# Layer 3's ConvFFN: fourteen of its twenty-two ktiles of up-projection as 2x2 blocks in seven products

## The chip, the core and the metric

The kernel runs on one core of a Trainium2 chip, in one launch. The metric is the device time of one execution in microseconds (us), lower is better. An execution's time is compared as a median over runs; the profile shows one further execution, instruction by instruction.

## The reference

Four layers work on 640 tokens (512 sample, 128 prompt) of 1024 features, each a token mixer and a gated ConvFFN, each of these followed by a LayerNorm. The change lies in the ConvFFN of layer 3, the last sub-layer of the program:

```python
def _conv_ffn(h, w_up, conv_w, conv_b, w_down):
    a, b = jnp.split(h @ w_up, 2, axis=-1)
    ap = jnp.pad(a, ((0, 0), (1, 1), (0, 0)))
    a = ap[:, :-2] * conv_w[0] + ap[:, 1:-1] * conv_w[1] + ap[:, 2:] * conv_w[2] + conv_b
    return (jax.nn.gelu(a) * b) @ w_down
```

`h` is 640 x 1024, `w_up` 1024 x 5632 (2816 for `a` and 2816 for `b`), `w_down` 2816 x 1024. The convolution runs over the tokens of each group for itself. All is float32.

## The kernel before

**Layout.** Features lie on the 128 partitions, tokens along the free dimension. A ktile is 128 features: 1024 features are 8 ktiles, the 2816 of the FFN are 22. Tokens are worked in halves, half 0 = tokens 0 to 256 and half 1 = 256 to 640 (in the very last projection 0 to 384 and 384 to 640).

**Split operands.** A float32 product is made of float32r parts: each operand is held as (hi, lo), and `mm3` (L175 to L177) issues three matmuls per ktile of the contraction, hi·hi (L175), hi·lo (L176) and lo·hi (L177), adding up in PSUM. Weights come by `unit`: SyncE's queue (SP) loads 512 KB into one of four buffers `raw`, ScalarE (ACT) casts it to the hi part (L163), VectorE (DVE) subtracts for the lo part (L164), both into one of six buffers `hl`:

```python
nc.scalar.copy(hl[:, 0], r)                                  # L163
(e or nc.vector).tensor_sub(hl[:, 1], r, hl[:, 0])           # L164
```

Activations are split in the same way by `split` (L169, L170).

**The FFN.** Ktile j of the up-projection needs two pieces of weights (2j for `a`, 2j+1 for `b`), each a contraction over 8 ktiles of h. `up(j)` makes four products: `a` of half 0 and 1, copied by ACT into a padded buffer `ap` (`ffn_a`, L500 to L503), and `b` of half 0 and 1. `ffn_g` then does the convolution (one ACT pass, L512, and two DVE passes, L514, for the sample and for the prompt each), gelu on ACT (L516), the product with `b` read from PSUM (DVE, L518 and L519) and the split of the result g. Of the first six ktiles half 0 is made earlier, in `ffn_pre`, while the LayerNorm of half 1 is still at work; `skew` makes their half 1, from ktile 5 down to ktile 0. Then `up(6)` and on. The down-projection runs in three chunks of ktiles, 0 to 7, 7 to 14 and 14 to 22: a chunk's `down` comes behind the first ktile of the next chunk, and the last chunk's `project` ends the program with the LayerNorm and the stores.

**What sets the order.** A scheduler places the instructions of this code when the program is built, by priority and by a model of durations; what comes out is one fixed list for each engine, which the engine works off in order, each instruction waiting on semaphores for what it reads and for the buffer that it writes. Buffers are handed on in pools: a new tile of `hl` takes the buffer of the oldest one, once all who read that are done. No DMA of the kernel before is issued from GpSimd's queue (POOL); every load goes through SP.

Of the kernel before, what the change touches and what calls it, by code (L numbers as in the profile page):

```python
# [1399 lines left out]
```

## Time and profile before

| | us |
|---|---|
| median of 3 runs (2803.19 to 2812.57) | 2807.13 |
| span of the profiled execution | 2805.7 |
| layer 3's ConvFFN: `skew`, from about | 2363 |
| its `up` and `down` in between | 2412 to 2738 |
| last chunk, LayerNorm and stores to | 2806 |

The profiled execution's own span is 1.4 us under the median. The page gives the busy time of each engine over the span; PE is TensorE's matmuls, PEld its weight loads, DVE VectorE, ACT ScalarE, POOL GpSimd. In a timeline an instruction stands with its start, its duration, the shapes, and in brackets how long the engine had been idle before it and what it waited for. Matmuls are pipelined: the distance between two starts is what one costs, the duration shown is from issue to the modelled end. "PEclk" in a table by windows is TensorE's granted clock as a share of full speed (1.00 is 2.4 GHz, 0.50 is 1.2 GHz).

### The profile page before, as it was taken

The page shows a single profiled execution, that of the slowest core. Times are in us where ns is not written, and L with a number is a line of the kernel's source. Part 1 is how long each engine was busy: PE and PEld are TensorE (multiplying, and loading weights), DVE is VectorE, ACT ScalarE, POOL GpSimd, SP SyncE. Part 2 cuts the span into 40 slices and gives each one's busy share as a digit, 9 for nine tenths or more (in the row PEclk, how much of TensorE's full clock was granted, in tenths as well). Part 3 has the DMA queues.
Part 4 walks back from the last instruction along what each step waited for, and adds up shares of the span by engine and source line. Part 5 has one row for each costly group of instructions (what it writes and reads, how often), then busy time and mean ns, then how long its engine had stood idle before and what let it go on. Part 6 is the DMA issues. An engine that isn't in the chain of part 4 may idle for free.

```text
span 2805.7 us, 46039 instructions
## 1 busy us (share of the span) xinstructions
PE 2749.6 (98%) x17826; PEld 2636.0 (94%) x17826; DVE 1973.0 (70%) x4263; ACT 1240.0 (44%) x2286; POOL 407.5 (15%) x417
## 2 busy tenths in 40 slices
PE   7999999999999999999999999999999999999998
PEld 4799999999989999999978999999799999999998
DVE  6879977857697887777587878775756558534344
ACT  5656232336496752323367423234532248423233
POOL 1250000024303300000442000005100042000003
PEclk9999999999999999999989999999999999999999
DMA  7735644432402445455104554542422224322221
GB/s 241 259 109 163 198 154 149 156 121 80 134 22 83 136 153 158 149 157 153 56 35 150 151 165 151 158 136 80 161 65 91 68 62 152 97 82 68 83 75 54
DMA packets 99932, 344.70 MB, mean 123 GB/s; under 512 B 11392, under 2 KB 14080, under 8 KB 99584
## 3 DMA queue, kind: packets, MB, share of 16 engines
q1 hardware_dynamic: 99712, 341.74, 38.7%
q8 instruction: 141, 2.31, 0.3%
q14 instruction: 79, 0.65, 0.1%
HBM read 336.19 MB, written 2.88 MB: 121 GB/s over the span
## 4 chain that ended last, share of the span: by engine, by line
PE 88%; DVE 5%; issue 2%; ACT 2%; DMA 2%; POOL 1%; POOLq 0%; ACTq 0%; SPq 0%; DVEq 0%
PE mm L175 26%; PE mm L176 26%; PE mm L177 26%; PE mm L487 2%; PE st L352 1%; PE mm L1157 1%; DVE hl L164 1%; DVE tmp L339 1%; DMA raw<-in_wmod 1%; PE mm L1247 1%; PE bc L372 1%; DVE lnt L383 1%; DVE act L170 0%; PE mm L1072 0%; DMA raw<-in_wup 0%
## 5 line engine op out<-in xcount | busy, mean ns | idle before, releaser
L177 PE MATMUL mm<-act,hl 128*128 128x384 f32 (+2 forms) x4928 | 1528.5, 310 | 3.2 <-DVE hl L164 3.2
L175 PE MATMUL mm<-act,hl 128*128 128x384 f32 (+2 forms) x4928 | 1531.5, 311 | 0.0
L176 PE MATMUL mm<-act,hl 128*128 128x384 f32 (+2 forms) x4928 | 1528.6, 310 | 1.2 <-POOL act L418 1.2
L177 PEld LDWEIGHTS mm<-act,hl 128*128 128x128 f32 x4928 | 935.1, 190 | 5.0 <-DVE hl L164 4.4
L176 PEld LDWEIGHTS mm<-act,hl 128*128 128x128 f32 x4928 | 935.9, 190 | 3.7 <-POOL act L418 1.8
L175 PEld LDWEIGHTS mm<-act,hl 128*128 128x128 f32 x4928 | 935.2, 190 | 3.2 <-ACT hl L163 0.6
L163 ACT CAST hl<-raw 128x1024 fp32r<-128x1024 f32 (+1 forms) x433 | 444.1, 1030 | 625.9 <-PE mm L177 560.1
L164 DVE TENSOR_TENSOR hl<-raw,hl 128x1024 fp32r<-128x1024 f32 (+1 forms) x428 | 526.0, 1231 | 67.4 <-ACT hl L163 65.1
L283 DVE SCALAR_TENSOR_TENSOR bc<-raw,cbc 128x512 f32<-128x512 f32 x608 | 406.2, 719 | 130.3 <-DMA raw<-in_wmod 130.0
L436 DVE SCALAR_TENSOR_TENSOR x<-mm,mod,x 128x256 f32<-128x256 f32 (+2 forms) x408 | 166.0, 434 | 200.4 <-PE mm L177 199.8
L514 DVE SCALAR_TENSOR_TENSOR tmp<-ap,vecs,tmp 128x512 f32<-128x512 f32 x352 | 170.5, 547 | 147.6 <-ACT tmp L512 147.4
L333 POOL TENSOR_TENSOR tmp<-x,tmp 128x256 f32<-128x256 f32 (+1 forms) x180 | 178.0, 993 | 153.2 <-DVE x L436 109.0
L527 POOL MEMSET ap<- 128x1 f32 x24 | 2.1, 99 | 1188.4 <-DVE tmp L514 735.3
L502 ACT COPY ap<-mm 128x256 f32<-128x256 f32 x88 | 33.0, 375 | 265.2 <-PE mm L177 265.2
L333 POOL TENSOR_TENSOR tmp<-x 128x256 f32<-128x256 f32 (+1 forms) x30 | 30.7, 1024 | 733.3 <-DVE x L436 694.5
L383 DVE TENSOR_TENSOR lnt<-x,bc 128x256 f32<-128x256 f32 (+1 forms) x240 | 109.6, 479 | 14.9 <-PE bc L372 14.4
L332 ACT ACTIVATE lnt<-x 128x256 f32<-128x256 f32 (+1 forms) x112 | 51.2, 467 | 133.3 <-DVE x L436 130.9
L516 ACT ACTIVATE tmp<-tmp 128x640 f32<-128x640 f32 x88 | 65.2, 740 | 100.4 <-DVE tmp L514 100.4
L169 ACT CAST act<-tmp 128x640 fp32r<-128x640 f32 x117 | 84.9, 726 | 52.1 <-DVE tmp L519 31.8
L512 ACT ACTIVATE tmp<-ap,vecs 128x512 f32<-128x512 f32 (+1 forms) x176 | 106.4, 658 | 0.0
L339 DVE TENSOR_TENSOR tmp<-tmp,lnt 128x384 f32<-128x384 f32 (+1 forms) x126 | 93.7, 745 | 14.1 <-ACT lnt L332 12.6
L487 PE MATMUL mm<-h,raw 128*128 128x256 f32 x416 | 101.2, 399 | 1.8 <-DVE lnt L404 1.8
(209 smaller groups left out, 2684.1 us busy)
## 6 DMA issues: line engine op xcount, KB each, us to landing
raw<-in_wup SPq DMA_DIRECT2D x216, 512.0 KB, 3.5
raw<-in_wmod SPq DMA_DIRECT2D x184, 512.0 KB, 3.5
raw<-in_wdn SPq DMA_DIRECT2D x64, 448.0 KB, 3.4
raw<-in_wdn SPq DMA_DIRECT2D x46, 512.0 KB, 3.6
raw<-in_wgv SPq DMA_DIRECT2D x24, 512.0 KB, 4.1
raw<-in_wgo SPq DMA_DIRECT2D x19, 512.0 KB, 3.9
raw<-in_wqk SPq DMA_DIRECT2D x18, 512.0 KB, 3.5
raw<-in_wgu SPq DMA_DIRECT2D x16, 512.0 KB, 3.5
```

What stands on the lines that cost most here:

```text
L163: nc.scalar.copy(hl[:, 0], r)
L164: (e or nc.vector).tensor_sub(hl[:, 1], r, hl[:, 0])
L175: t.matmul(out, lhs[0], rhs[0], start=start, stop=False)
L176: t.matmul(out, lhs[0], rhs[1], start=False, stop=False)
L177: t.matmul(out, lhs[1], rhs[0], start=False, stop=stop)
L283: nc.vector.scalar_tensor_tensor(out=self.bc(), in0=r[:, sl], scalar=1.0, in1=self.cbc[:, g, sl], op0=ALU.mult, op1=ALU.mult, accum_out=ac ...
L333: nc.gpsimd.tensor_add(S.s[0], z, S.s[0] if n > 1 else S.first)
L339: (self.nc.gpsimd if S.pool else self.nc.vector).tensor_add(S.s[1], S.s[1], S.last)
L383: self.nc.vector.tensor_sub(t, self.x[:, k, a:b], MU)
L436: nc.vector.scalar_tensor_tensor(out=self.x[:, m, s0:s1], in0=ps[:, s0 - a:s1 - a], scalar=sc, in1=self.x[:, m, s0:s1], op0=ALU.mult, op1= ...
L487: self.nc.tensor.matmul(ps, w[:, k, :], h32[:, k, :], start=k == 0, stop=k == NK - 1)
L514: nc.vector.scalar_tensor_tensor(out=c[:, sl], in0=ap[:, o + i:o + i + n], scalar=cw(i), in1=c[:, sl], op0=ALU.mult, op1=ALU.add)
```

## The change

Only layer 3's ConvFFN computes in another way (`SEVEN`); in layers 0 to 2 the order of TensorE's instructions is as it was.

- `up(6)` and `up(7)` stay plain. Ktiles 8 to 21 go through the new `up7(j)`. It sees the product of one ktile as a 2x2 block product: on the weights' side a and b by the two halves of the contraction (4 ktiles each), on the right side those two halves by tokens 0 to 320 and 320 to 640. Seven products of sums take the place of eight (the arrangement of Winograd), each of 4 ktiles x 3 matmuls of 320 columns: 84 matmuls a ktile, where `up` has 48 of 256 and 48 of 384 columns.
- On the weights' side each ktile needs sums, made by four DVE additions of 128x512 into a tile `sums` of the `hl` pool, and four split tiles: wA (the raw a), wB and wC (of the sums) and wD (half of b). On the right side the operands are made once, by `seven_pre`, in eight steps of DVE additions and splits: one behind each of the ktiles 3 to 0 of `skew` and two behind each of `up(6)` and `up(7)`.
- Products land in three PSUM tiles X, Y, Z; three of them are kept in SBUF by ACT copies, and DVE additions put a and b together. `ffn_g` with `neg` does the convolution over 641 columns in one piece, and the sign of b in its last pass.
- A remainder (lo) is made in a second way, `halves(..., dma=True)`: ACT writes hi, ACT writes minus hi, and a DMA issued from POOL's queue adds the raw weights to it. So for wA and wC, and for every piece of weights of layer 3 in `skew`, `up(6)` and `up(7)`. wB and wD keep the DVE subtraction.
- The chunks of layer 3 are 0 to 6, 6 to 11, 11 to 15 and 15 to 22. The pool of activations has 18 buffers (16 before), `hl` has 7 (6 before); a constant moves into an `hl` buffer, and the scratch for DMA descriptors is set to 4096.

```diff
-FFN_CHUNKS = ((0, 7), (7, 14), (14, 22))
+FFN_CHUNKS = {None: ((0, 7), (7, 14), (14, 22)), 3: ((0, 6), (6, 11), (11, 15), (15, 22))}
...
+SEVEN = {None: NJ, 3: 8}
+HT = T // 2
...
-        self.actp = P("actp", 16)
-        self.hlp = P("hlp", 6)
+        self.actp = P("actp", 18)
+        self.hlp = P("hlp", 7)
...
+    def halves(self, hl, r, e=None, dma=False):
+        nc = self.nc
         nc.scalar.copy(hl[:, 0], r)
+        if dma:
+            nc.scalar.activation(hl[:, 1], r, AF.Copy, scale=-1.0)
+            nc.gpsimd.dma_start(hl[:, 1].bitcast(F32), r, accum_op=ALU.add)
+        else:
+            (e or nc.vector).tensor_sub(hl[:, 1], r, hl[:, 0])
...
         def wu(i):
-            return self.unit(a["wup"][L, i], [128, NK, 128])
+            return self.unit(a["wup"][L, i], [128, NK, 128], dma=at(SEVEN, L) < NJ)
...
                 gs[j] = self.ffn_g(L, j, ap, t[:, 1], bB)
+                if j < 4:
+                    steps(pre7, 1)
...
+        def seven_pre():
...
+            for k in range(4):
...
+                v.tensor_sub(w, up[:, :, A], up[:, :, B])
+                v.tensor_add(w[:, 0], w[:, 0], w[:, 1])
+                self.split(room[0], w[:, 0])
+                v.tensor_sub(z, lo[:, :, B], up[:, :, B])
+                v.tensor_add(z[:, 0], z[:, 0], z[:, 1])
+                self.split(room[1], z[:, 0])
+                yield
...
+        def up7(j, ops):
...
+            S = self.hlp.tile([128, 16, 128], F32, tag="hl", name=self.nm("sums"))
+            v.tensor_add(S[:, 4:8], b1, b2)
+            v.tensor_add(S[:, 0:4], a1, b1)
+            v.tensor_add(S[:, 8:12], a1, S[:, 4:8])
+            v.tensor_add(S[:, 12:16], a2, S[:, 8:12])
+            wA, wB, wC, wD = new(), new(), new(), new(4)
+
+            self.halves(wA, ra, dma=True)
+            self.halves(wB, S[:, 8:16])
+            self.halves(wC, S[:, 0:8], dma=True)
+            self.halves(wD, b2)
+            X, Y, Z = self.mm([128, HT]), self.mm([128, HT]), self.bc([128, HT])
...
+            prod(X, wA, 0, ops[0], True)
+            r1 = keep(X)
+            prod(Y, wA, 4, ops[1], True)
+            v.tensor_add(ap[:, 1:1 + HT], r1, Y)
...
+            prod(X, wB, 0, ops[2], False)
+            r2 = keep(X)
+            prod(Z, wC, 4, ops[3], True)
+            m5 = keep(Z)
...
+            prod(X, wC, 0, ops[4], False)
+            v.tensor_add(m5, m5, X)
+            prod(Z, wB, 4, ops[5], False)
+            v.tensor_add(ap[:, 1 + HT:513], r2[:, 0:512 - HT], Z[:, 0:512 - HT])
+            v.tensor_add(ap[:, 514:642], r2[:, 512 - HT:HT], Z[:, 512 - HT:HT])
...
+            prod(X, wD, 0, ops[6], False)
...
+            gs[j] = self.ffn_g(L, j, ap, X, m5, neg=True)
...
             for j in range(max(k0, at(SKEW, L)), k1):
-                up(j)
+                if j >= at(SEVEN, L):
+                    if ops is None:
+                        ops = next(pre7)
+                    up7(j, ops)
+                else:
+                    up(j)
+                    steps(pre7, 2)
```

**Three places in the order.** First ACT's list where `skew` goes from ktile 2 to ktile 1. Before: tmp3760 is the gelu of ktile 2 and act3762 its g, mm3767 the first product of ktile 1, and hl3784 and hl3793 are weights of ktiles further on.

```order
L516 ACTIVATE tmp3760_24667<-tmp3760_24667 128x640
L163 CAST hl3784_24842<-raw3783_24840 128x1024
L169 CAST act3762_24678<-tmp3761_24675 128x640
L502 COPY ap1_105<-mm3767_24692 128x256
L503 COPY ap1_105<-mm3767_24692 128x128
L512 ACTIVATE tmp3769_24744<-ap1_105,vecs_82 128x512
L512 ACTIVATE tmp3769_24744<-ap1_105,vecs_82 128x128
L163 CAST hl3793_24964<-raw3792_24962 128x1024
```

After, at the same place: act3768 is the g of ktile 2, act3756 a right operand of `seven_pre`, and hl3770, hl3772 and hl3781 are the weights of the next three products (L172 writes hi, L174 minus hi).

```order
L545 ACTIVATE tmp3766_24688<-tmp3766_24688 128x640
L181 CAST act3768_24699<-tmp3767_24696 128x640
L181 CAST act3756_24611<-tmp3759_24614 128x320
L172 CAST hl3770_24710<-raw3769_24708 128x1024
L174 ACTIVATE hl3770_24710<-raw3769_24708 128x1024
L172 CAST hl3772_24716<-raw3771_24714 128x1024
L174 ACTIVATE hl3772_24716<-raw3771_24714 128x1024
L172 CAST hl3781_24799<-raw3780_24797 128x1024
```

The cast of ktile 1's first weights stood well ahead of ktile 2's g, and now stands behind it, and the adding DMA behind that cast.

TensorE's list at this place, after; mm3765 is the last product of ktile 2.

```order
L189 MATMUL mm3765_24663<-act3607_23531,hl3763_24631 128x384
L187 MATMUL mm3773_24721<-act3600_23524,hl3770_24710 128x384
L188 MATMUL mm3773_24721<-act3600_23524,hl3770_24710 128x384
L187 MATMUL mm3774_24748<-act3600_23524,hl3772_24716 128x384
L188 MATMUL mm3774_24748<-act3600_23524,hl3772_24716 128x384
L187 MATMUL mm3784_24810<-act3600_23524,hl3781_24799 128x384
L188 MATMUL mm3784_24810<-act3600_23524,hl3781_24799 128x384
L189 MATMUL mm3773_24721<-act3600_23524,hl3770_24710 128x384
```

Six matmuls that read only hi parts are drawn ahead; the first that reads a lo part (L189 of mm3773) stands behind them. Before, the products followed one another here in the order of the code.

Second, ACT's list where `up(7)` ends and `up7(8)` begins. act3845 is the g of ktile 7, op3846 and act3603 are right operands; hl3852, hl3853 and hl3854 are wA, wB and wC of ktile 8, sums3851 its sums.

```order
L181 CAST op3846_25525<-tmp3847_25526 128x320
L181 CAST op3846_25525<-tmp3848_25527 128x320
L181 CAST act3845_25522<-tmp3844_25519 128x640
L181 CAST op3846_25525<-tmp3848_25527 128x320
L172 CAST hl3852_25559<-raw3849_25550 128x1024
L174 ACTIVATE hl3852_25559<-raw3849_25550 128x1024
L181 CAST act3603_23527<-op3757_24612 128x320
L172 CAST hl3853_25560<-sums3851_25554 128x1024
L172 CAST hl3854_25561<-sums3851_25554 128x1024
```

Before, ACT's list at such a place, around a plain `up` (mm3850 and mm3851 are its a, act3856 its g; hl3880 and hl3882 are weights of the next piece):

```order
L500 COPY ap1_105<-mm3850_25642 128x256
L502 COPY ap1_105<-mm3851_25668 128x256
L503 COPY ap1_105<-mm3851_25668 128x128
L512 ACTIVATE tmp3854_25745<-ap1_105,vecs_82 128x512
L512 ACTIVATE tmp3854_25745<-ap1_105,vecs_82 128x128
L163 CAST hl3880_26015<-raw3879_26013 128x1024
L516 ACTIVATE tmp3854_25745<-tmp3854_25745 128x640
L163 CAST hl3882_26020<-raw3881_26018 128x1024
L169 CAST act3856_25756<-tmp3855_25753 128x640
```

The casts of the next weights stood ahead of the split of g; now the first weights of the next ktile stand behind it. TensorE's list has four hoisted matmuls here (two each of ktile 8's first two products), ahead of the first that reads hl3852's lo part.

Third, ACT's list within the seven-product ktiles, here from ktile 17 to 18, with the semaphores that each instruction waits for (DMASW is an adding DMA of POOL's queue, DMAHW a load). lnt4067 and lnt4068 keep the products r1 and r2 of ktile 17, act4056 is the g of ktile 16, hl4076 to hl4078 are wA, wB and wC of ktile 18; hl4076 lies in the buffer in which the sums of ktile 17 were.

```order
L716 COPY lnt4067_27368<-mm4064_27353 128x320 [waits PE_49]
L528 ACTIVATE tmp4054_27318<-tmp4054_27318 128x641 [waits DVE_49]
L172 CAST hl4076_27471<-raw4073_27462 128x1024 [waits DMAHW5_49,DMASW1_49,Activation_49]
L174 ACTIVATE hl4076_27471<-raw4073_27462 128x1024
L181 CAST act4056_27327<-tmp4055_27323 128x640 [waits DVE_49]
L716 COPY lnt4068_27395<-mm4064_27353 128x320 [waits PE_49]
L716 COPY lnt4069_27409<-bc4066_27355 128x320 [waits PE_49]
L172 CAST hl4077_27472<-sums4075_27466 128x1024 [waits DVE_49,PE_49]
L172 CAST hl4078_27473<-sums4075_27466 128x1024 [waits PE_49]
L174 ACTIVATE hl4078_27473<-sums4075_27466 128x1024
```

Ktiles 9, 10, 13, 14 and 17 to 20 stand so, eight of the fourteen: the cast of wA (here hl4076) waits for the adding DMA that reads the sums of the ktile before, and behind it stands the copy of r2, whose PSUM tile the next product but one writes again.

## Rows read from the trace of the kernel before

**Rows 1.** The page: the span; busy time, share and instructions of each engine.
```profile
span 2805.7 us, 46039 instructions
...
PE 2749.6 (98%) x17826; PEld 2636.0 (94%) x17826; DVE 1973.0 (70%) x4263; ACT 1240.0 (44%) x2286; POOL 407.5 (15%) x417
```

**Rows 2.** PE's waits, whole run: total us, times, longest us.
```profile
PE mm L177 <- DVE hl L164: 3.2, 4, 1.7
...
PE mm L487 <- DVE lnt L404: 1.8, 1, 1.8
...
PE mm L175 <- DVE msq L814: 1.2, 1, 1.2
```

**Rows 3.** Windows: busy us (x) of PE, PEld, DVE, ACT, POOL; PEclk, DMA, GB/s.
```profile
2412.00:2637.00 225.00, 225.00 (x1538) 225.00 (x1537) 90.95 (x147) 63.97 (x98) 0.00 (x0) 1.00 0.26 79
```

**Rows 4.** Timeline of PE: one product of 384 and one of 256 columns.
```profile
2403.83 0.33 PE L175 MATMUL mm<-act,hl 128*128 128x384 f32 x1
...
2410.42 0.33 PE L177 MATMUL mm<-act,hl 128*128 128x384 f32 x1
2410.59 0.28 PE L175 MATMUL mm<-act,hl 128*128 128x256 f32 x1
...
2412.62 0.28 PE L177 MATMUL mm<-act,hl 128*128 128x256 f32 x1
```

**Rows 5.** Timeline of PE, layer 1: 320-column matmuls, start and duration.
```profile
772.39 0.31 PE L175 MATMUL mm<-act,act 128*128 128x320 f32 x1
...
773.57 0.31 PE L177 MATMUL mm<-act,act 128*128 128x320 f32 x1
```

**Rows 6.** Groups by form, 2412:2738: shapes, count, busy us, mean ns, idle before.
```profile
L164 DVE TENSOR_TENSOR hl<-raw,hl 128x1024 fp32r<-128x1024 f32 x34 | 41.6, 1223 | 9.9 <-ACT hl L163 9.9
L163 ACT CAST hl<-raw 128x1024 fp32r<-128x1024 f32 x34 | 35.6, 1046 | 94.8 <-PE mm L177 94.8
L514 DVE SCALAR_TENSOR_TENSOR tmp<-ap,vecs,tmp 128x512 f32<-128x512 f32 x32 | 24.0, 749 | 86.9 <-ACT tmp L512 86.9
...
L170 DVE TENSOR_TENSOR act<-tmp,act 128x640 fp32r<-128x640 f32 x17 | 13.9, 819 | 0.0
...
L169 ACT CAST act<-tmp 128x640 fp32r<-128x640 f32 x17 | 12.3, 723 | 0.0
...
L519 DVE TENSOR_TENSOR tmp<-tmp,mm 128x384 f32<-128x384 f32 x16 | 8.9, 554 | 38.1 <-PE mm L177 38.1
...
L500 ACT COPY ap<-mm 128x256 f32<-128x256 f32 x16 | 6.0, 376 | 20.8 <-PE mm L177 20.8
```

**Rows 7.** DMA issues, 2400:2740: count, KB each, median us to landing.
```profile
raw<-in_wup SPq DMA_DIRECT2D x28, 512.0 KB, 3.4
```

**Rows 8.** DMA issues, 690:780, from tile to tile.
```profile
tmp<-act SPq DMA_DIRECT2D x39, 64.0 KB, 2.0
```

**Rows 9.** Timeline of ACT in skew.
```profile
2394.15 1.05 ACT L163 CAST hl<-raw 128x1024 fp32r<-128x1024 f32 x1
2395.18 0.73 ACT L169 CAST act<-tmp 128x640 fp32r<-128x640 f32 x1
```

**Rows 10.** Timeline of PE at the start: idle time and what ended it.
```profile
22.45 0.58 PE L269 MATMUL bc<-identr,tmp 2*128 2x2 f32 x4 [4.16 <-DVE tmp L266]
```

**Rows 11.** Windows behind that wait (columns of rows 3).
```profile
26.00:27.00 1.00, 0.80 (x2) 0.27 (x2) 0.31 (x2) 1.00 (x2) 1.00 (x2) 0.50 0.00 0
27.00:28.00 1.00, 1.00 (x4) 0.66 (x4) 0.63 (x1) 0.63 (x1) 0.33 (x1) 0.79 0.23 66
```

**Rows 12.** Timeline of PE: one of the waits of rows 2.
```profile
2347.42 0.38 PE L177 MATMUL mm<-act,hl 128*128 128x256 f32 x1 [1.73 <-DVE hl L164]
```

**Rows 13.** Windows behind it (columns of rows 3).
```profile
2350.00:2352.00 2.00, 2.00 (x12) 2.00 (x12) 2.00 (x3) 1.05 (x2) 0.00 (x0) 0.52 0.67 207
```

**Rows 14.** Timeline of DVE: a subtraction of 128x1024.
```profile
2364.29 1.57 DVE L164 TENSOR_TENSOR hl<-raw,hl 128x1024 fp32r<-128x1024 f32 x1
```

**Rows 15.** Timeline of POOL at the same time.
```profile
2363.76 1.02 POOL L418 TENSOR_TENSOR act<-lnt,act 128x384 fp32r<-128x384 f32 x1 [1.58 <-ACT act L417]
```

More of the change, by code (lines that the diff above doesn't have):

```diff
@@ L170, in split, with mm3 @@
         (e or self.nc.vector).tensor_sub(dst[:, 1], src, dst[:, 0])
-    def mm3(self, out, lhs, rhs, start, stop):
+    def mm3(self, out, lhs, rhs, start, stop, on=False):
         t = self.nc.tensor
-        t.matmul(out, lhs[0], rhs[0], start=start, stop=False)
-        t.matmul(out, lhs[0], rhs[1], start=False, stop=False)
-        t.matmul(out, lhs[1], rhs[0], start=False, stop=stop)
+        t.matmul(out, lhs[0], rhs[0], start=start, stop=False, skip_group_check=on)
+        t.matmul(out, lhs[0], rhs[1], start=False, stop=False, skip_group_check=on)
+        t.matmul(out, lhs[1], rhs[0], start=False, stop=stop, skip_group_check=on)
     def vec(self, col, n=1):
@@ L614, in down @@
                     self.bg(at(BG, L))
+        def seven_pre():
+            acts = [self.act([128, 2, 2, HT]) for _ in range(3)]
+            n1, n2, t3 = [], [], []
+            t4 = None
+            v = nc.vector
+            fl = lambda x: x.bitcast(F32)
+            A, B = slice(0, HT), slice(HT, T)
+            for k in range(4):
+                if k < 2:
+                    room = [acts[k][:, 0], acts[k][:, 1], acts[2][:, k]]
+                else:
+                    t = self.hlp.tile([128, 3, 2, HT], F32R, tag="hl", name=self.nm("op"))
+                    room = [t[:, i] for i in range(3)]
+                if t4 is None:
+                    t4 = self.hlp.tile([128, 4, HT], F32, tag="hl", name=self.nm("op"))
+                up, lo = fl(hs[k][:, :, :]), fl(hs[k + 4][:, :, :])
+                w, z = self.tmp([128, 2, HT]), self.tmp([128, 2, HT])
+                v.tensor_sub(w, up[:, :, A], up[:, :, B])
[5 more added lines that the diff above has]
+                yield
+                v.scalar_tensor_tensor(out=z[:, 0], in0=z[:, 0], scalar=-1.0, in1=up[:, 0, A], op0=ALU.mult, op1=ALU.subtract)
+                v.tensor_sub(z[:, 0], z[:, 0], up[:, 1, A])
+                self.split(room[2], z[:, 0])
+                v.scalar_tensor_tensor(out=z[:, 0], in0=z[:, 0], scalar=-1.0, in1=lo[:, 0, A], op0=ALU.mult, op1=ALU.subtract)
+                v.tensor_sub(t4[:, k], z[:, 0], lo[:, 1, A])
+                for o, r in zip((n1, t3, n2), room):
+                    o.append(r)
+                yield
+            for k in range(4):
+                self.split(hs[k][:, :, HT:T], t4[:, k])
+            b = lambda k, sl: (hs[k][:, 0, sl], hs[k][:, 1, sl])
+            pair = lambda t: (t[:, 0], t[:, 1])
+            yield ([b(k, slice(0, HT)) for k in range(4)], [b(k + 4, slice(0, HT)) for k in range(4)],
+                   [pair(t) for t in n2], [pair(t) for t in n1], [pair(t) for t in t3],
+                   [b(k + 4, slice(HT, T)) for k in range(4)], [b(k, slice(HT, T)) for k in range(4)])
@@ new lines, in up7, with prod, keep @@
+        def up7(j, ops):
+            v = nc.vector
+            ra, rb = self.raw_unit(a["wup"][L, 2 * j]), self.raw_unit(a["wup"][L, 2 * j + 1])
+            new = lambda n=8: self.hlp.tile([128, 2, n, 128], F32R, tag="hl", name=self.nm("hl"))
+            a1, a2, b1, b2 = ra[:, 0:4], ra[:, 4:8], rb[:, 0:4], rb[:, 4:8]
+            S = self.hlp.tile([128, 16, 128], F32, tag="hl", name=self.nm("sums"))
[9 more added lines that the diff above has]
+            X, Y, Z = self.mm([128, HT]), self.mm([128, HT]), self.bc([128, HT])
+            def prod(ps, w, k0, rhs, first):
+                for k in range(4):
+                    self.mm3(ps, (w[:, 0, k0 + k], w[:, 1, k0 + k]), rhs[k], first and k == 0, k == 3, not first)
+            def keep(ps):
+                t = self.small("lnt", [128, HT], LNT)
+                nc.scalar.copy(t, ps)
+                return t
+            ap = self.aps[j % 2]
+            prod(X, wA, 0, ops[0], True)
+            r1 = keep(X)
+            prod(Y, wA, 4, ops[1], True)
+            v.tensor_add(ap[:, 1:1 + HT], r1, Y)
+            self.bg(at(BG, L))
+            prod(X, wB, 0, ops[2], False)
+            r2 = keep(X)
+            prod(Z, wC, 4, ops[3], True)
+            m5 = keep(Z)
+            self.bg(at(BG, L))
+            prod(X, wC, 0, ops[4], False)
[3 more added lines that the diff above has]
+            v.tensor_add(ap[:, 514:642], r2[:, 512 - HT:HT], Z[:, 512 - HT:HT])
+            self.bg(at(BG, L))
+            prod(X, wD, 0, ops[6], False)
+            self.bg(at(BG, L))
+            gs[j] = self.ffn_g(L, j, ap, X, m5, neg=True)
```

37 lines of the change are left out of this document (28 added, 9 removed).

## The prediction

> **What bounds the kernel now.** First the page: TensorE is busy in 2749.6 of 2805.7 us, VectorE in 1973.0, ScalarE in 1240.0 [rows 1]. Then the table by windows: through the up- and down-projections of the last FFN (2412 to 2637, and the same to 2738) PE is busy in all of the window at a granted clock of 1.00, while DVE is busy in 91 of 225 us, ACT in 64, POOL in none, and DMA uses a quarter of its engines [rows 3]. PE's waits over the whole run are few and short, and none lies in that stretch [rows 2]. So the stretch is as long as its matmuls, columns saved there are time saved, and any wait that the change brings to PE is time lost. DVE and ACT are free for more than half of it, and they cost nothing until PE waits for them in a place.
>
> **What the change saves.** A 384-column matmul starts 0.1734 us behind the one before (2403.83 to 2410.42 over 38), a 256-column one 0.1194 (2410.59 to 2412.62 over 17) [rows 4], so a plain ktile takes 48 x 0.1734 + 48 x 0.1194 = 14.05. A 320-column one takes 0.1475 (772.39 to 773.57 over 8) [rows 5], so a ktile in seven products takes 84 x 0.1475 = 12.39, 1.77 a product. Fourteen ktiles save 14 x 1.66 = **23.2 us**. This holds at a clock of 1.00.
>
> **What lies beside it.** Per ktile DVE gets four sums of 128x512 (about half of the 1.22 of a 1024 subtraction [rows 6] each), a subtraction of 1024 and one of 512, three or four additions (about 0.5 each), two convolution passes and the product and split of g: about 9.6 of the 12.4 us. ACT gets six passes of 1024 or 512, 5.9, three copies of 320 columns (0.4 each) and the passes of g, about 9.5. Both fit, so I cost them at nothing as volume; what covers them is PE's 12.4 us a ktile. The sixteen more evacuations of a fourth chunk run on DVE under `down`, where it is idle for long, the right operands on DVE and ACT under `skew`. The loads stay at two of 512 KB a ktile, 3.4 us each [rows 7], and pools, scratch and the moved constant cost nothing. If this cover went, PE would wait for the excess of the longer engine; it is not near. What costs is the order.
>
> **The unknown: the adding DMA.** The trace has no DMA issued by POOL. Call its time L, from issue to landing, for 512 KB between tiles. A load of 512 KB takes 3.4 [rows 7], a move of 64 KB between tiles 2.0 [rows 8]; so 448 KB cost 1.4, 512 KB about 1.6, and 1.8 are fixed. The lower bound is 3.4, as a load. An addition reads the source and what it adds to, and writes: with each of three passes at 1.6, the upper bound is 1.8 + 4.8 = 6.6. I take 1.8 + 2 x 1.6 = **5.0**, for two reads; the nearest row (the load) speaks for the lower end, the doubled reading for more. POOL itself is idle in the stretch [rows 3], so its queue starts at once. Where `before` had a DVE subtraction of 1.22 us [rows 6] behind ACT's cast, there is now a pass of ACT (1.03) and then L.
>
> **Wait one: `skew`, ktile 2 to 1.** In the order of before, the weights of ktile 1 are cast a ktile ahead. In that of after, ACT first has the g of ktile 2 to split, which is there only when DVE has multiplied it by ktile 2's last product. From that product's end: 0.3 of the matmul's tail [rows 4], 0.55 the DVE product, 0.72 ACT's split [rows 6], 0.37 the split of a right operand, 1.03 the cast [rows 9], 1.03 minus hi; at 4.0 the DMA is issued, at 4.0 + L it lands. Only the six hoisted matmuls of 384 columns run meanwhile, 1.04. PE waits 2.95 + L = **8.0**. It would be some 6 even with a quick DMA, as hi parts of two further pieces of weights stand behind on ACT.
>
> **Wait two: `up(7)` to `up7(8)`.** The split of ktile 7's g and of a last right operand stand ahead of the cast of wA. On DVE: tail 0.3, product 0.5, three steps of 320 columns at 0.4, subtraction of g 0.75, one more step 0.45 = 3.2; on ACT 0.4, 1.03 and 1.03 = 5.7, then L; less four hoisted matmuls, 0.6. PE waits 5.1 + L = **10.1**. Behind the cast on ACT stand all other weights of ktile 8; they are late too, but later needed.
>
> **The steady waits.** In eight ktiles wA of the next ktile lies in the buffer of this one's sums, which is free when the adding DMA of wC has read them. Follow it from the start of product 0: wC's cast waits for the end of product 5 of the ktile before, 1.77 earlier, and needs two passes, 2.06, with handovers 2.3; so the DMA is issued at 0.53 and lands at 0.53 + L. Then ACT makes wA (two passes, 2.0), the split of the last g (0.65) and the copy of r2 (0.4), with handovers 3.15 in all. Product 4 overwrites r2's tile and should start at 4 x 1.77 = 7.08; the copy is done at 3.68 + L. PE waits L - 3.4 = 1.6, eight times: **12.8**. Of the other six ktiles two follow a down-projection and one follows wait two, with the buffer long free; in three only product 3 waits, when L is over 5.1. Before, ACT's list had casts two pieces ahead of use, and its only long waits were for PE itself [rows 6].
>
> **Small and the clock.** At the first down-projection, g of the last ktile of the chunk is needed at once: 1.2, as one of the waits of before [rows 2]. After a wait TensorE ran at its lower level: behind the wait of 4.16 us that ended at 22.45 [rows 10] the granted clock was 0.50 until 27 and back at 1.00 after 28 [rows 11]. Some 5.3 us at half speed lose 2.65. The two long waits cost 2 x 2.65 = **5.3**. Short waits are mixed: one of 1.73 [rows 12] was followed by windows at 0.52 to 0.62 [rows 13], about 1.7 lost; those of 1.2 and less were mostly not. The steady waits, 1.6 each, lie at that edge. Between none of eight and all of them (13.6), I take two: **3.4**.
>
> **Sum.** -23.2 + 8.0 + 10.1 + 12.8 + 1.2 + 5.3 + 3.4 = +17.6. The execution profiled has a span of 2805.7 [rows 1], 1.4 under the median of 2807.1; 2807.1 + 17.6 = 2824.7, so **2825**. With L from 4.6 (waits 7.55 + 9.7 + 9.6, clock 1.7 for the steady ones) to 5.8 (8.75 + 10.9 + 19.2, product 3 another 2.1, clock 8) the sum runs from +12 to +33: 2819 to 2840, the forecast's own range.
>
> **Rival: the adding DMA is as quick as a load.** Then L = 3.4, the steady waits are zero, the two long ones 6.35 and 8.5, and with 1.2 and 5.3 the sum is -1.9: **2805**, no change; without loss of clock 2800. It speaks for it that the tile-to-tile move and the load agree in fixed cost, and that DMA is three quarters idle [rows 3]; against it, that the addition must read twice. It decides below L = 4.2. On this the Trainium skill, page "DMA: Bandwidth & Descriptors", section "Anatomy of one DMA — SWDGE (gpsimd) path", gives 2.0 us plus the bytes at 436 GB/s for a DMA issued by GpSimd: an estimate of 3.2 us for 512 KB, without a word on addition; the sum by it would be about -2.3. No run so far shows such a DMA.
>
> **Rival: POOL's part is held up by DVE.** DVE is busy three quarters of a seven-product ktile, mostly with two operands from SBUF. Where such a subtraction met an instruction of POOL it took 1.57 where the mean is 1.22 [rows 6, 14, 15]: the two engines get in each other's way. If the making of the DMA does too, it starts one DVE pass later, L is 6.0 to 6.5: waits 9.0 to 9.5, 11.1 to 11.6, 20.8 to 24.8, product 3 another 2.7 to 4.2, clock 13.6 as the steady waits are then well over 1.7. The sum is +41 to +47: **2848 to 2854**. Against it: the making is short, and DVE has gaps. The Trainium skill, page "SBUF — State Buffer", section "Who interferes with whom", says that such DMAs starve only while DVE holds the shared write port, which an addition of two tensors does not; by it this rival falls, and the sum stays.
>
> **Rival: quicker than a load.** If moving within the chip's own memory costs only the fixed part and a bit, L = 2.4, steady waits gone, and if the clock did not fall behind the long waits, the sum is -23.2 + 5.4 + 7.5 + 1.2 = -9.1: **2798**, faster. The first long wait's floor and rows 10 speak against it.
>
> That the change doesn't do what it says is hardly a case: the order shows 84 matmuls of 320 columns in every ktile from 8.
>
> **Chances.** About 0.3% (8.4 us) is what a measurement of this kernel can tell from no change. The forecast 0.47, slower by more than that; as quick as a load 0.26, within it; held up by DVE 0.18, slower; quicker than a load 0.09, faster. Faster 0.09, same 0.26, slower 0.65. The range goes from 2800 (a load's L without loss of clock) to 2846 and leaves out the last rival and about half of the second.
>
> **What would show it.** A stretch of matmuls 12.4 us long from product 0 to product 0 in the ktiles behind a down-projection (12 and 16), and about 14 in 9, 10, 13, 14, 17 to 20. Two waits of PE of 7 to 11 us for a lo part written by DMA, at ktile 1 and ktile 8, each followed by windows at 0.50. Eight waits for ACT's copy (L716), 1.6 each. In the DMA table, `hl<-raw` of 512 KB on POOL's queue at about 5.0. I am wrong if L is below 4.2 or above 6, if ACT's passes are much longer on the sums, or if one engine's 9.6 us a ktile turns out at over 12.4, which would stretch every ktile alike.

## The result and the profile after

The changed kernel took 2826.3 us (median of 4 runs, 2824.7 to 2827.4) where the kernel before took 2805.2 (2802.7 to 2812.6): ratio 1.0075, 95% interval 1.006 to 1.009. It is slower, by 21 us. The forecast was 2825.

Of the page: the span, the engines' busy time, and the DMA queue of POOL, which had no row before.

```profile
span 2822.9 us, 46139 instructions
...
PE 2735.7 (97%) x17658; PEld 2612.9 (93%) x17658; DVE 2032.7 (72%) x4428; ACT 1307.9 (46%) x2366; POOL 440.8 (16%) x459
...
q0 software_dynamic: 6048, 22.02, 4.3%
```

PE is busy for 14 us less than in [rows 1] and the span is 17 us longer: matmuls went away, and waiting came. (The profiled execution reached layer 3's `skew` 4.5 us earlier than that of the kernel before, for reasons that lie in the layers ahead; from the first matmul of `skew` to the end it took 467.6 us against 445.9, which is 21.7 more and agrees with the medians.)

The DMA issues of layer 3's FFN (line of the issue: KB each, median us from issue to landing), which answer to [rows 7]:

```profile
raw<-in_wup SPq DMA_DIRECT2D x36, 512.0 KB, 3.9
hl<-raw POOLq DMA_DIRECT2D x26, 512.0 KB, 4.6
hl<-sums POOLq DMA_DIRECT2D x14, 512.0 KB, 5.0
```

By these medians an adding DMA of 512 KB takes 4.6 us on raw weights and 5.0 on the sums. They are the L of the prediction, taken as 5.0. One by one they spread more: 4.5 where nothing else is in flight, 4.7 for the sums of the steady ktiles (a load starts 2 us behind the issue there), 7.7 and 7.9 for the sums of ktiles 8 and 9, where two loads run beside each, and 4.6, 5.6, 8.1 and 10.8 for the four that `skew` issues from 2395.0 to 2400.7.

The waits of PE that were not in [rows 2] (total us, times, longest):

```profile
PE mm L187 <- ACT hl L172: 13.4, 7, 4.8
...
PE bc L189 <- DMA hl<-sums: 7.7, 7, 2.7
...
PE mm L187 <- ACT lnt L716: 6.7, 7, 1.1
...
PE mm L189 <- DMA hl<-raw: 5.3, 2, 4.3
```

The lines have moved with the code: L172 is ACT's cast of weights, L174 minus hi, L181 and L182 the split of activations, L189 the matmul that reads the lo part of weights, L716 ACT's copy of a product. The two long waits, in PE's timeline (start, duration, and in brackets the idle time and what ended it), first at `skew`'s ktile 1, then at ktile 8:

```profile
2393.80 0.69 PE L187 MATMUL mm<-act,hl 128*128 128x384 f32 x1 [3.30 <-ACT hl L172]
...
2395.69 0.69 PE L187 MATMUL mm<-act,hl 128*128 128x384 f32 x1 [0.89 <-ACT hl L172]
...
2397.58 0.69 PE L187 MATMUL mm<-act,hl 128*128 128x384 f32 x1 [0.89 <-ACT hl L172]
...
2399.59 0.69 PE L189 MATMUL mm<-act,hl 128*128 128x384 f32 x1 [1.00 <-DMA hl<-raw]
```

```profile
2494.21 0.63 PE L187 MATMUL mm<-act,hl 128*128 128x320 f32 x1 [4.84 <-ACT hl L172]
...
2499.99 0.63 PE L189 MATMUL mm<-act,hl 128*128 128x320 f32 x1 [4.35 <-DMA hl<-raw]
```

They stand where the order had them: a few hoisted matmuls on hi parts that come one by one as ACT casts them, then one that needs a lo part and waits for the adding DMA. 6.1 us are idle at the first, 9.2 at the second. Around them, windows with PE's clock as the third number from the end:

```profile
2394.00:2396.00 2.00, 1.11 (x3) 0.61 (x4) 0.71 (x2) 2.00 (x3) 0.85 (x1) 0.50 0.00 0
...
2402.00:2404.00 2.00, 2.00 (x8) 2.00 (x8) 0.00 (x0) 0.00 (x0) 0.00 (x0) 0.50 0.91 182
2404.00:2406.00 2.00, 2.00 (x13) 2.00 (x12) 0.00 (x0) 0.00 (x0) 0.00 (x0) 0.99 1.03 272
...
2500.00:2502.00 2.00, 2.00 (x7) 2.00 (x8) 0.69 (x1) 0.23 (x1) 0.87 (x1) 0.50 0.43 102
...
2694.00:2700.00 6.00, 4.86 (x33) 4.56 (x32) 3.69 (x8) 3.87 (x6) 0.86 (x1) 1.00 0.55 145
```

From 2394 to 2404 the granted clock is 0.50, and again at ktile 8 until 2503; in 2694 to 2700, where PE waits 1.1 us, it stays at 1.00.

How long each ktile took, worked out from the starts of the 320-column matmuls, from a ktile's first product to the end of its seventh, in us (ktile 8 also has 5.0 of waiting ahead of its first matmul):

| ktile | 8 | 9 | 10 | 11 | 12 | 13 | 14 | 15 | 16 | 17 | 18 | 19 | 20 | 21 |
|---|---|---|---|---|---|---|---|---|---|---|---|---|---|---|
| changed | 20.6 | 17.3 | 14.5 | 13.2 | 12.3 | 13.9 | 14.0 | 13.3 | 12.4 | 13.9 | 14.0 | 14.0 | 12.8 | 14.2 |
| e1 | 20.2 | 14.9 | 13.3 | 13.4 | 12.3 | 12.4 | 13.6 | 13.1 | 12.7 | 12.4 | 13.4 | 13.7 | 13.9 | 13.4 |
| e4 | 18.0 | 12.3 | 12.3 | 12.3 | 12.3 | 12.3 | 12.3 | 12.3 | 12.3 | 12.3 | 12.3 | 12.3 | 12.3 | 12.3 |
| e6 | 13.8 | 14.0 | 13.4 | 13.6 | 12.3 | 12.4 | 13.4 | 13.2 | 13.0 | 12.4 | 14.2 | 14.2 | 13.8 | 13.4 |

The rows e1, e4 and e6 belong to the experiments below. A plain ktile was 14.05, so nearly all that the seven products save in ktiles 13, 14 and 17 to 19 is lost again in the same ktile.

The chain of waits that ended last, in one such ktile (start, us, what):

```profile
2703.46 4.72 DMA hl<-sums
2708.34 1.05 ACT hl L172
2709.39 0.92 ACT hl L174
...
2710.86 0.42 ACT lnt L716
2711.33 0.41 PE mm L187
2715.15 1.05 ACT hl L172
2716.20 0.97 ACT hl L174
2717.45 4.71 DMA hl<-sums
2722.32 1.05 ACT hl L172
```

This is a ring. The adding DMA of wC of one ktile lands at 2708.2; then come ACT's cast of the next wA, its minus hi, the split of g and the copy of r2; PE's product 4 begins at 2711.3; ACT's cast of the next wC waits until PE has done that product and the one behind it, which frees a buffer, and at 2717.4 the next adding DMA is issued. One turn takes 13.98 us.

### The profile page after: what moved, and what is told of

Same layout as the page of the kernel before. It is cut to its first block, busy times and chain, and to the rows that moved or that the text cites. A ratio compares the mean times of both kernels' runs of the same rounds, so it can differ in the third digit from the quotient of the medians.

```text
span 2822.9 us, 46139 instructions
## 1 busy us (share of the span) xinstructions
PE 2735.7 (97%) x17658; PEld 2612.9 (93%) x17658; DVE 2032.7 (72%) x4428; ACT 1307.9 (46%) x2366; POOL 440.8 (16%) x459
## 5 line engine op out<-in xcount | busy, mean ns | idle before, releaser
L187 PE MATMUL mm<-act,hl 128*128 128x384 f32 (+3 forms) x4704 | 1465.4, 312 | 17.6 <-ACT hl L172 10.8
L189 PE MATMUL mm<-act,hl 128*128 128x384 f32 (+3 forms) x4704 | 1459.6, 311 | 8.4 <-DMA hl<-raw 5.3
L188 PE MATMUL mm<-act,hl 128*128 128x384 f32 (+3 forms) x4704 | 1460.4, 311 | 2.8 <-POOL act L432 1.9
L187 PEld LDWEIGHTS mm<-act,hl 128*128 128x128 f32 x4704 | 892.7, 190 | 25.5 <-ACT hl L172 13.6
L189 PEld LDWEIGHTS mm<-act,hl 128*128 128x128 f32 x4704 | 891.6, 190 | 11.9 <-DMA hl<-raw 6.6
L188 PEld LDWEIGHTS mm<-act,hl 128*128 128x128 f32 x4704 | 893.4, 190 | 6.2 <-POOL act L432 3.5
L172 ACT CAST hl<-raw 128x1024 fp32r<-128x1024 f32 (+4 forms) x441 | 439.1, 1000 | 568.7 <-PE mm L189 455.3
L177 DVE TENSOR_TENSOR hl<-raw,hl 128x1024 fp32r<-128x1024 f32 (+4 forms) x408 | 484.3, 1190 | 57.7 <-ACT hl L172 54.7
L450 DVE SCALAR_TENSOR_TENSOR x<-mm,mod,x 128x256 f32<-128x256 f32 (+2 forms) x432 | 175.9, 435 | 186.2 <-PE mm L189 185.7
L543 DVE SCALAR_TENSOR_TENSOR tmp<-ap,vecs,tmp 128x512 f32<-128x512 f32 (+1 forms) x296 | 143.7, 546 | 77.3 <-ACT tmp L541 77.1
L397 DVE TENSOR_TENSOR lnt<-x,bc 128x256 f32<-128x256 f32 (+1 forms) x240 | 109.7, 479 | 15.4 <-PE bc L386 13.9
L181 ACT CAST act<-tmp 128x640 fp32r<-128x640 f32 (+1 forms) x123 | 87.4, 712 | 58.4 <-DVE tmp L548 34.5
L182 DVE TENSOR_TENSOR act<-tmp,act 128x640 fp32r<-128x640 f32 (+1 forms) x123 | 98.6, 804 | 21.8 <-ACT act L181 21.2
L353 DVE TENSOR_TENSOR tmp<-tmp,lnt 128x384 f32<-128x384 f32 (+1 forms) x126 | 93.4, 742 | 13.8 <-ACT lnt L346 12.3
L545 ACT ACTIVATE tmp<-tmp 128x640 f32<-128x640 f32 x74 | 54.7, 740 | 101.9 <-DVE tmp L543 101.9
L410 ACT ACTIVATE x<-lnt,vecs 128x256 f32<-128x256 f32 (+1 forms) x128 | 82.2, 648 | 27.7 <-DVE lnt L409 26.9
```

Source lines behind the costliest of these rows:

```text
L187: t.matmul(out, lhs[0], rhs[0], start=start, stop=False, skip_group_check=on)
L188: t.matmul(out, lhs[0], rhs[1], start=False, stop=False, skip_group_check=on)
L189: t.matmul(out, lhs[1], rhs[0], start=False, stop=stop, skip_group_check=on)
L397: self.nc.vector.tensor_sub(t, self.x[:, k, a:b], MU)
L450: nc.vector.scalar_tensor_tensor(out=self.x[:, m, s0:s1], in0=ps[:, s0 - a:s1 - a], scalar=sc, in1=self.x[:, m, s0:s1], op0=ALU.mult, op1= ...
L543: nc.vector.scalar_tensor_tensor(out=c[:, sl], in0=ap[:, o + i:o + i + n], scalar=cw(i), in1=c[:, sl], op0=ALU.mult, op1=ALU.add)
```

## The experiments

Theory at the start: the two long waits come from the order on ACT, the steady ones from the adding DMA's time in a ring through the buffer of the sums, with the copy of r2 on ACT as the link to PE. Each kernel below is the changed one with the edit shown; times are medians, compared with runs of the kernel before on the same chip (2803.9 to 2805.0).

**e1: r2 kept by VectorE.**

```diff
-            r2 = keep(X)
+            r2 = self.small("lnt", [128, HT], LNT)
+            v.tensor_copy(r2, X)
```

> The kept copy of the third product (r2) is made by VectorE instead of ScalarE; nothing else is changed. Theory (ScalarE's queue is the link: the copy stands behind the cast of wA, which waits for the adding DMA that reads the sums): PE's waits for ScalarE's copy (seven, 6.7 us in the changed kernel) go; ktiles 13, 14, 17, 18, 19 fall from 13.9 to 14.0 us to about 12.4; the whole falls by 9 to 12 us against the changed kernel, to about 2815. Rival (the adding DMA itself or the weights' loads pace these ktiles): they stay at 13.5 to 14 us, and the wait moves to a remainder written by DMA; the whole stays at 2824 to 2827.

2821.9 us (ratio 1.0056, 1.0041 to 1.0071): 4 us off, not 9 to 12. The waits for ACT's copy are gone, but these are the waits of PE (total, times, longest) now:

```profile
PE bc L189 <- DMA hl<-sums: 9.3, 9, 2.3
...
PE mm L189 <- DMA hl<-raw: 6.4, 3, 4.4
```

Ktiles 13 and 17 fall to 12.4, as the theory had it; 14 and 18 to 20 are at 13.4 to 13.9. The chain of waits in one of them:

```profile
2698.52 5.79 DMA hl<-sums
...
2704.47 1.05 ACT hl L172
2705.52 0.95 ACT hl L174
2706.48 0.62 ACT act L181
...
2707.13 0.82 DVE act L182
2707.95 0.61 DVE sums L701
...
2708.64 2.06 ACT hl L172 x2
2710.70 0.97 ACT hl L174
...
2711.95 6.07 DMA hl<-sums
```

From one adding DMA of wC to the next it is 13.4 us, and PE isn't in the chain at all: the landing (5.8), the next wA's cast and minus hi, the split of g on ACT and VectorE, the last of the next sums, which stands behind that split in VectorE's list, two casts and minus hi. The result lies between the theory and the rival. The copy of r2 was one link; with it gone another branch of the same ring is nearly as long. In this turn loads of SP's queue run beside the adding DMA from its issue on, and it lands in 5.8 where the changed kernel has 4.7; with 4.7 the turn would be an estimated 12.4.

**e4, e7, e8: the remainders of wA and wC by subtraction.** e4 has both edits, e7 the second alone, e8 the first alone.

```diff
-            self.halves(wA, ra, dma=True)
+            self.halves(wA, ra)
...
-            self.halves(wC, S[:, 0:8], dma=True)
+            self.halves(wC, S[:, 0:8])
```

> wA and wC of the seven-product ktiles get their remainders by VectorE's subtraction, not by adding DMAs; skew and the two plain ktiles keep theirs. VectorE then has some 12 us of work in a ktile of 12.4. Theory (what costs in these ktiles is the adding DMA's time in the loop of buffers): all of ktiles 9 to 21 at 12.3 to 12.6, the second wait at ktile 8 (4.4) some 1.2 to 3 shorter; the whole falls by 15 to 20 us, to about 2808. Rival (VectorE is then the bound): ktiles at 12.8 to 13.5 everywhere, also in 12 and 16, which are 12.3 in the changed kernel; the whole falls by less than 10.

2802.8 us (0.9996, 0.9986 to 1.0005): 23.5 us under the changed kernel, more than the 15 to 20 expected, and level with the one before. Every ktile from 9 to 21 takes 12.32. The window of ktiles 16 to 21 (PE, PEld, DVE, ACT, POOL busy; clock):

```profile
2662.56:2736.50 73.94, 73.94 (x506) 73.94 (x506) 62.73 (x102) 42.93 (x60) 0.00 (x0) 1.00 0.28 90
```

PE waits for nothing in these 73.9 us and VectorE is busy for 62.7 of them: near, and not the bound. The rival is out. At ktile 8 only the second wait is shorter:

```profile
2495.07 0.64 PE L187 MATMUL mm<-act,hl 128*128 128x320 f32 x1 [4.83 <-ACT hl L172]
...
2499.28 0.63 PE L189 MATMUL mm<-act,hl 128*128 128x320 f32 x1 [2.77 <-DVE hl L177]
```

> The changed kernel with one edit: wC's remainder by VectorE's subtraction; wA keeps its adding DMA. Theory (the loop runs through wC's DMA, which holds the sums): ktiles 9 to 21 at 12.3 to 12.5, waits at ktile 8 kept (4.8 and 4.4); the whole falls by 18 to 21 us against the changed kernel, to about 2806. Rival (either adding DMA paces the ktiles): ktiles at 13 or more, 2814 or more.

2805.3 us (1.0002, 0.9993 to 1.0012), ktiles 9 to 21 at 12.32, as the theory said. The one adding DMA left in a ktile, on raw weights, lands in 4.5.

> The changed kernel with one edit: wA's remainder by VectorE's subtraction; wC keeps its adding DMA. Theory (the loop runs through wC's DMA): still waits of PE for the remainder of the sums, ktiles at 12.8 to 13.5 where they follow one another, the second wait at ktile 8 shorter by 1.5; 2812 to 2818. Rival (the loop is only too long because two adding DMAs a ktile slow each other): wC's DMA lands in under 5 us, ktiles at 12.3 to 12.5, 2805.

2807.6 us (1.0013, 1.0002 to 1.0024), ktiles 9 to 21 at 12.3 to 13.0, most at 12.4. The theory's 12.8 to 13.5 was too long. The rival's time is nearer, but not its reason: in the steady ktiles of the changed kernel the two adding DMAs never run at once (2710.6 to 2715.2 and 2717.5 to 2722.2 in the turn above), and the one on the sums mostly takes 4.7 to 4.8 in either kernel. What shortened the ring stands in ACT's timeline behind that landing:

```profile
2690.16 1.05 ACT L172 CAST hl<-raw 128x1024 fp32r<-128x1024 f32 x1 [1.18 <-DMA hl<-sums]
2691.11 0.42 ACT L716 COPY lnt<-mm 128x320 f32<-128x320 f32 x1
2691.43 0.73 ACT L181 CAST act<-tmp 128x640 fp32r<-128x640 f32 x1
```

The pass for minus hi (0.96) is gone, and the scheduler now places the copy of r2 ahead of the split of g (0.62), which so leaves the ring too: 13.98 - 0.96 - 0.62 = 12.4. The ring closes in time, or nearly so, with either of the two adding DMAs taken out.

**e11: each adding DMA in two halves.** A dose: the ring is to follow the landing.

```diff
-            nc.gpsimd.dma_start(hl[:, 1].bitcast(F32), r, accum_op=ALU.add)
+            for q in (slice(0, 4), slice(4, 8)):
+                nc.gpsimd.dma_start(hl[:, 1, q].bitcast(F32), r[:, q], accum_op=ALU.add)
```

> Each adding DMA of 512 KB is issued as two of 256 KB, one behind the other on POOL's queue. Theory (the loop of buffers follows the time of the adding DMA): whichever way the pair's landing moves, ktiles 13, 14, 17 to 19 move with it: if moving bytes is most of its 4.6 to 5.0 us, the halves overlap, the pair lands within 0.3 us of the one and the ktiles stay at 13.6 to 14.2; if each DMA has its own fixed part and its own 0.86 us of POOL one after the other, the pair lands 0.9 to 1.5 later, ktiles at 14.5 to 15.5, the whole at 2838 to 2850. Rival (the ktiles are set by something else): ktiles at 14.0 though the pair lands later.

2845.0 us in a single run. ACT's timeline of one turn, between ktiles 18 and 19 (L174 is minus hi, whose end lets POOL issue):

```profile
2705.37 1.05 ACT L172 CAST hl<-raw 128x1024 fp32r<-128x1024 f32 x1 [3.41 <-DMA hl<-sums]
...
2712.18 1.05 ACT L172 CAST hl<-sums 128x1024 fp32r<-128x1024 f32 x1 [0.71 <-PE bc L190]
2713.14 1.05 ACT L174 ACTIVATE hl<-sums 128x1024 fp32r<-128x1024 f32 x1
...
2721.69 1.05 ACT L172 CAST hl<-raw 128x1024 fp32r<-128x1024 f32 x1 [3.59 <-DMA hl<-sums]
```

From the end of minus hi (2714.2) to the cast that waits for the pair it is 7.5 us, where the changed kernel has 5.2 (2717.2 to 2722.3); the turn is 16.32 where it was 13.98. Landing and turn grow by the same 2.3 us, more than the 0.9 to 1.5 expected, and the ring's other part is 8.8 in both: it follows the landing, and the rival is out.

**e2, e9: `skew`'s weights ahead of g, or split by subtraction.** e2 asks for the next ktile's weights ahead of `ffn_g`; e9 has `dma=False` in `wu`.

```diff
                 bB = self.up_mm(hs, wb, 1)
                 self.bg(at(BG, L))
+                if 0 < j < 4 and L == 3:
+                    nxt = [wu(u) for u in (2 * j - 2, 2 * j - 1)]
                 gs[j] = self.ffn_g(L, j, ap, t[:, 1], bB)
```

> In skew the weights of the next ktile are asked for in the code ahead of the last steps of the ktile before (g, right operands) for ktiles 3 to 1; adding DMAs and all else stay. Theory (the cast of ktile 1's weights stands behind ktile 2's g in ScalarE's list): the stretch of 288 matmuls of 384 columns falls from 62.0 to 51 to 54 us (50.7 before the change), no long wait at ktile 1, no half clock there; the whole falls by 8 to 11 us, to about 2816. Rival (the adding DMA's 4.6 us in place of VectorE's 1.2 us subtraction is what makes skew slow): the wait stays at 5 us or more at some ktile and the stretch over 57.

> The changed kernel, with the weights of skew and of the two plain ktiles split by VectorE's subtraction as before the change; their order and all else stay. It is the fourth corner beside the changed kernel (late and adding: 62.0 us for skew's 288 matmuls), e2 (ahead and adding: 55.8) and e5 (ahead and subtracting: 51.3). Theory (the cast behind g is the larger part, the adding DMA and the passes for minus hi the smaller): the first wait at ktile 1 stays (3.4), the others shrink to about 1.2 together, the half clock stays: 57 to 59. Rival (the adding DMA is the larger part): under 55.

e2 took 2820.1 us (1.0053, 1.0036 to 1.0071), 6 us off where 8 to 11 were expected, and e9 2823.4 in a single run. The stretch of `skew`'s 288 matmuls, from the starts in PE's timeline (50.7 in the kernel before):

| `skew`, us | adding DMA | subtraction |
|---|---|---|
| weights behind g | 62.0 (changed) | 58.4 (e9) |
| weights ahead of g | 55.8 (e2) | 51.3 (e5, and e6 below) |

Both count: the order is worth 6.2 to 7.1, the adding DMA with its pass for minus hi 3.6 to 4.5. In e2 one wait for a remainder is left, and in e9 the wait for the cast with a short one for VectorE behind it:

```profile
2400.53 0.44 PE L189 MATMUL mm<-act,hl 128*128 128x384 f32 x1 [2.44 <-DMA hl<-raw]
```

```profile
2396.40 0.69 PE L187 MATMUL mm<-act,hl 128*128 128x384 f32 x1 [3.42 <-ACT hl L172]
...
2398.54 0.69 PE L189 MATMUL mm<-act,hl 128*128 128x384 f32 x1 [0.51 <-DVE hl L177]
```

The theory's range for e2 (51 to 54) was too low; it named the larger cause and left out the smaller. e9 came out as its theory had it.

**e3: ktile 8's sums and wA ahead of ktile 7's g.** The loads, sums and wA of ktile 8 move into a function `first`, called in `up(7)`; the last four steps of the right operands go into the first `down`.

```diff
             bB = self.up_mm(hs, wb, 1)
             self.bg(at(BG, L))
+            got = first(j + 1) if j == at(SEVEN, L) - 1 and L == 3 else None
             gs[j] = self.ffn_g(L, j, ap, bA, bB)
...
                     self.evac(ps, L, 5, m, half)
                     self.bg(at(BG, L))
+                if k0 == 0 and m % 2 == 0:
+                    steps(pre7, 1)
```

> The sums and wA of ktile 8 are asked for ahead of ktile 7's last steps, and the last four steps of the right operands lie in the first down-projection instead of behind ktiles 6 and 7. Theory (order on ScalarE and VectorE makes ktile 8 late): the two waits at ktile 8 (4.8 and 4.4 us) go, with the half clock behind them; from the end of ktile 7's matmuls to the end of ktile 8 some 13 us instead of 25.6; the whole falls by 11 to 14 us, to about 2814. Rival (the right operands, whose last parts are also needed there, are late by themselves): the wait only moves to an operand and the whole falls by less than 5.

2812.6 us (1.0025, 1.0013 to 1.0037), 14 us off, as expected. Both waits at ktile 8 are gone, ktile 8 takes 13.9 with no idle time ahead of it; `skew` and the steady ktiles are as in the changed kernel. The two edits, wA's place and the right operands' place, are not told apart.

**e10: the chunks and pools alone.**

```diff
-SEVEN = {None: NJ, 3: 8}
+SEVEN = {None: NJ}
```

> The changed kernel with the seven products and the adding DMAs off: plain ktiles, but four chunks, 18 buffers of activations, 7 of weights, the moved constant. Theory (these cost next to nothing): 2803 to 2808, no wait of PE over 0.3 us between skew and the last projection, ktiles at 14.05. Rival (chunks or buffers cost): 2809 or more.

2807.1 us (1.0009, 0.9999 to 1.0018), no wait of PE over 0.3 us from `skew` to the last projection. Four chunks, larger pools and the moved constant cost nothing that can be told from the noise (5 us at most by the interval).

**e5, e6: all three places mended.** e5 joins e1, e2, e3, e4 and e9; e6 is the same with the adding DMAs of wA and wC left in.

> No adding DMA anywhere in the FFN (all remainders by VectorE's subtraction), weights of the next ktile ahead of g in skew, sums and wA of ktile 8 ahead of ktile 7's last steps, the right operands' last four steps in the first down-projection, r2 kept by VectorE. Theory (the seven products save 14 x 1.73 = 24 us, and all that was lost lies in the three places and the adding DMAs): no long wait of PE from skew to the last ktile, all ktiles at 12.3, skew at 51 to 52; 2805 - 24 + 2 = 2783 (2780 to 2788). Rival (part of the loss lies elsewhere: chunks, buffers, VectorE near its bound): 2790 or more, with ktiles over 12.6 or a new wait.

> As e5_ahead_subtract, but wA and wC of the seven-product ktiles get their remainders by adding DMAs, as in the changed kernel. Theory (a loop of buffers through wC's adding DMA, the next sums and their casts paces these ktiles, as with r2 on VectorE alone): ktiles 13 to 14 us where they follow one another, waits of PE for a remainder of the sums of 0.7 to 1.5; 8 to 16 us more than e5, 2792 to 2799. Rival (with the starts in order, the adding DMAs find room): within 3 us of e5.

e5 took **2784.0 us** (2780.5 to 2784.5; ratio 0.9919, 0.9903 to 0.9936): 21 us under the kernel before and 42 under the changed one. It is the fastest. Its window over ktiles 16 to 21, columns as above:

```profile
2642.30:2716.20 73.90, 73.90 (x506) 73.90 (x505) 64.86 (x108) 40.31 (x54) 0.00 (x0) 1.00 0.30 89
```

PE never waits there; VectorE is at 88%. e6 took 2800.5 us (0.9982, 0.9972 to 0.9991), so in an otherwise mended kernel the two adding DMAs of a ktile cost 16.5 us in all, a little over the range expected. Their landings there, with loads beside those on the sums:

```profile
hl<-sums POOLq DMA_DIRECT2D x14, 512.0 KB, 5.7
hl<-raw POOLq DMA_DIRECT2D x13, 512.0 KB, 4.5
```

## Why the prediction was right, point by point

**Where the time is bound.** Right: PE's matmuls set the end before, and every wait that came showed in the span.

**The saving.** 23.2 forecast, with 12.39 a ktile; undisturbed ktiles take 12.32, so it is 14 x 1.73 = 24.2. e5 gets 21 of it in the whole.

**The volume on VectorE and ACT at nothing.** Right, and e4 shows it with two more subtractions of 1.2 us a ktile on VectorE.

**The adding DMA at 5.0.** It measured 4.6 and 5.0 as medians, and in the three places where the sum used it 4.55 (`skew`), 4.54 (ktile 8) and 4.72 (the steady ktiles). The nearest row, the load at 3.4, would have been too low, and three passes (6.6) too high. That one number does for all places is not borne out: beside other traffic it took up to 10.8. By the Trainium skill's estimate for a DMA issued by GpSimd (page "DMA: Bandwidth & Descriptors", section "Anatomy of one DMA — SWDGE (gpsimd) path"), 3.2 us, the steady waits would have been nil. The trace disagrees: no adding DMA of the changed kernel landed in under 4.49.

**Wait one with its clock**, 8.0 + 2.65 = 10.7: the stretch of `skew` grew by 11.3. From the end of ktile 2's matmuls to the first that reads a lo part it took 9.3 us (2390.3 to 2399.6), where the prediction has 8.0 and 1.04 of hoisted matmuls; that is 8.2 lost. Only 6.1 of it shows as idle time, for the hoisted matmuls ran at half clock. The other 3.0 is mostly the half clock behind, until 2404. **Wait two with its clock**, 10.1 + 2.65 = 12.8: from the end of ktile 7's matmuls (2489.2) to the end of ktile 8 (2514.8) it took 25.6, that is 13.2 over a free ktile: 10.2 by the same count until the first lo part is read, and 3.0 behind it, of which 1.25 is a wait of product 3 that the prediction had not counted at ktile 8. **The start of the first down-projection**, 1.2: from `up(6)` to the end of `up(7)` 71.9 us for 70.3 us of matmuls, 1.6.

**The steady waits**, 12.8, and their share of lost clock, 3.4. Ktiles 9 to 21 took 19.5 over 13 x 12.32. The size in the five clean ones (13, 14 and 17 to 19) is right: the prediction's L - 3.4 with the 5.17 that the trace shows from the end of minus hi to the next cast gives 1.77, measured 1.6 to 1.7. Three terms of this step were mis-sized. Ktiles 11, 15 and 21 lost 0.9, 1.0 and 1.9, mostly by waits of product 3 (0.8, 1.0 and 1.0), which was to wait only above 5.1: the adding DMAs there took 5.6, 5.6 and 6.1, so the rule held and the single L of 5.0 did not. Ktile 9 lost 5.0, with a wait of 2.7 for the sums' remainder and half clock behind it, since ktile 8 had started everything late; ktile 20 lost 0.5 only. And the clock did not fall behind waits of 1.1: the 3.4 set for that went in ktile 9 alone, in which it cost about 1.7 (0.94 and 0.63 granted in two windows of 4 us).

What was incomplete is the mechanism: the prediction hung the steady wait on the copy of r2 in ACT's queue. The waits for that copy came, of 0.9 to 1.1 us in ktiles 10, 13, 14 and 17 to 19, six of the eight. But e1 took this link out, and of the clean ktiles only 13 and 17 came free; the others stayed at 13.4 and more, because the ring has a second branch, through the split of g and the sums. The cause is the adding DMA's time within a ring that has no slack (8.8 + 5.2 against 12.3), as e7 and e11 show, and not the copy's place.

**The sum.** Measured: -24.2 + 11.3 + 13.2 + 1.6 + 19.5 + 0.5 (the last projection with the LayerNorm) = +21.9, forecast +17.6. That the forecast time is off by 1.3 us only is in part luck: the sum was 4.3 too small by the trace (3.6 by the medians), and the median of before that it was added to 2.0 too high. (The upper end of the prediction's own range adds up to +32, not +33.)

**The rivals.** A DMA as quick as a load, and one quicker: out by the landing times. POOL held up by VectorE: out, since the issue on POOL took the same time all through (min/median/max in ns, the first numbers behind the colon):

```profile
L175 POOL DMA_DIRECT2D hl<-raw x28: 850/859/1050, 2347.9 to 2739.2; - x28
L175 POOL DMA_DIRECT2D hl<-sums x14: 859/859/869, 2500.2 to 2744.3; - x14
```

Sixteen of these 42 issues ran beside an operation of VectorE with two operands from SBUF; all of the sixteen but the very first of the run (1.05) took 0.85 to 0.87. This is what the Trainium skill's rule (page "SBUF — State Buffer", section "Who interferes with whom") had it come to for two-tensor additions, and the trace agrees. The landing does depend on other DMA traffic: 4.5 with nothing beside it, 5.7 on the sums in e6, with loads beside it.

## What to carry over

Where an engine in front has no slack, cost a new operation by the ring of buffers that it lies in, not by the engine it frees: a remainder by DMA took VectorE's 1.2 us off an engine that had time and put 5 us into a ring of 12.3. When one link of such a ring is taken out and the time stays, look for the next branch of it and change the long member. At a change of regime, ask for the first operands of the new one ahead of the last steps of the old: two such places (11.3 and 13.2 us, the adding DMA's part in `skew` included) cost as much as fourteen ktiles saved (24.2).
